# A trunk step on one core: the first twelve outputs of the first feed-forward stage summed in four quarters of the k tiles

## The chip, the cores and the metric

The kernel runs on one core of a Trainium2 chip. The metric is the device time of one execution in microseconds. The core has a matrix engine (TensorE, rows "PE", with its weight loads as "PEld"), a vector engine (VectorE, "DVE"), a scalar engine (ScalarE, "ACT"), GpSimd ("POOL") and a queue engine (SyncE, "SP"), on which nearly all transfers from memory are issued.

## What is computed

Two layers of a trunk over 256 tokens (128 of a context group, 128 of a latent group, d = 1024). A layer has three sub-layers: a feed-forward (SwiGLU, 2816 wide), a token mixer, and a second feed-forward; each is modulated by a condition and ends with a layer norm. The part at stake is the very first sub-layer:

```
mod = (silu(c) @ ada_w + ada_b)            # 9 rounds of 1024 columns per layer
h   = x * (1 + mod[scale]) + mod[shift]    # modulate
gate, up = split(h @ ffn1_w_in)            # k = 1024 = 8 tiles of 128
y   = (silu(gate) * up) @ ffn1_w_out
```

## The kernel before

**Work units.** The big products are a list of units, each up to 128x1024 of weights (512 KB), made by `_units` (line 129) and `_ffn_units` (line 47). In the first feed-forward unit ("g", f) holds the 8 k tiles of gate output f, ("u", f) those of up output f. A unit is loaded into one of 4 "raw" buffers (`ensure_dma`), split into a rounded part "hi" (ACT, line 520) and a rest "lo" (DVE, line 482) by `ensure_split`, and multiplied by `mmA`, which issues three TensorE instructions per k tile: hi with the rounded input, hi with its rest, lo with the rounded input. So a unit of 8 k tiles is 24 instructions. Five hi and five lo buffers let the split run three units ahead (`LEAD`).

**Start.** `setup` loads the condition, the 16 modulation tiles of the first two rounds (512 KB each, 16 buffers) and x in four pieces. `ada_start(q, A)` makes the modulation of two k tiles out of four modulation tiles: `strips` multiplies each as it comes, 8 products of 128 columns a tile on four 32-column strips of the array (bank D); then a copy by ACT, a transpose on TensorE (bank C), an add and a scale step on DVE. `build_u` then modulates x and splits it, per k tile. `first_four` runs the first four units k tile by k tile (four banks side by side), so that it can begin when two k tiles of the input are there; from the fifth unit on, a unit runs all its 8 k tiles in one go.

**Order.** Nothing runs in the order in which the code records it. `Program.order` is a list scheduler over all recorded operations with hand-set costs: a transfer of n bytes takes n/350 ns in one pipe after 1300 ns, and 700 ns more until it counts as landed; a TensorE product takes 109 ns; an operation with less time left until it is needed ("late") goes first. SP is free again 60 ns after an issue, so that in the plan a load is issued as soon as its buffer is free. What comes out is a fixed order for each engine, kept by the chip.

**Background work.** The other modulation rounds are partly summed on DVE ("d" pieces: two passes over a 128x1024 tile with the condition's row, line 486), from slot `D0` on; their row load (1 MB, `load_rows`) is issued at slot `GATE`, their tiles one slot each after that (`more_ada`), the rest of the constants at slot `GATE_C` (`late_loads`); all these loads wait for the newest "lo" (`gated`). The "k" pieces are strips on TensorE, some of them at the end of a sub-layer while the layer norm runs.

Of the kernel before, what the change touches and what calls it, by code (L numbers as in the profile page):

```python
# [16 lines left out]
P = 128  # L17
L = 2
D = 1024
KT = 8  # L20
# [22 lines left out]
def _r(c0, n=P):  # L43
    return list(range(c0, c0 + n))


def _ffn_units(s):
    wi, wo = f"ffn{s}_w_in", f"ffn{s}_w_out"
    k8 = list(range(KT))
    for f in range(FT):  # L50
# [78 lines left out]
def _units():  # L129
    out = []  # L130
    for l in range(L):
        for seq in (_ffn_units(1), _mix_units(), _ffn_units(2)):
# [122 lines left out]
DEP_ANY = 200  # L255
# [5 lines left out]


class Op:
    __slots__ = ("eng", "dur", "fn", "deps", "succ", "late", "due", "chain", "left", "ready", "nbytes", "pad")

    def __init__(self, eng, dur, fn, chain, due, nbytes, pad):
        self.pad = pad
        self.eng, self.dur, self.fn, self.chain, self.due, self.nbytes = eng, dur, fn, chain, due, nbytes
        self.deps, self.succ = set(), []
        self.late, self.left, self.ready = 1e18, 0, 0.0  # L270


class Program:
# [76 lines left out]
    def order(self):  # L350
# [15 lines left out]
        for i in range(len(ops) - 1, -1, -1):  # L366
            op = ops[i]
            late = end
            for j in op.succ:
                late = min(late, ops[j].late - _lat(op.eng, ops[j].eng))  # L370
            if not op.chain:
                k = bisect.bisect_right(slots, op.due)
                if k < len(slots) and first[slots[k]] > i:
                    late = min(late, ops[first[slots[k]]].late)
            op.late = late - op.dur
        free, now, later = {}, {}, {}
        for e in ("PE", "DVE", "ACT", "SP", "POOL"):
            free[e], now[e], later[e] = 0.0, [], []
# [6 lines left out]
        while len(out) < len(ops):  # L385
# [51 lines left out]
def _n(ap):  # L437
    n = 1
    for _, c in ap.ap[1:]:
        n *= c  # L440
    return n


class Recorder:
# [17 lines left out]
    def strips(self, items, start, stop):  # L462
        def fn():
            for out, lhsT, rhs in items:
# [3 lines left out]
        dur = sum(2 * max(107, _n(rhs) / 1.2) for _, _, rhs in items) / 4 + 70  # L468
        self.prog.add("PE", dur, fn, [x for _, a, b in items for x in (a, b)],
                      [o for o, _, _ in items] + ["strips"])  # L470
# [54 lines left out]
    def load(self, out, in_, queue="SP"):  # L525
        q = self.nc.sync if queue == "SP" else self.nc.gpsimd
        self.prog.add(queue, 60, lambda: q.dma_start(self.real(out), self.real(in_)), self.gate, [out], P * WORD * _n(out))

    def store(self, out, in_, queue="POOL"):
        q = self.nc.sync if queue == "SP" else self.nc.gpsimd  # L530
# [28 lines left out]
MIX_B = 60  # L559
MIXD_A = 48  # L560
MIXD_B = 80
D0 = 7


class Trunk:
# [106 lines left out]
    def ensure_dma(self, i):  # L672
        while self.n_dma <= min(i, len(self.units) - 1):
            k = self.n_dma
            n = self.units[k][3]
            self.raw[k] = self.t("raw", [UNIT])
            src = self.io["w"][self.offs[k]:self.offs[k + 1]].rearrange("(p n) -> p n", p=P)
            for a, b in self.cuts(k, n):
                self.nc.load(self.raw[k][:, a:b], src[:, a:b])
            self.n_dma += 1  # L680

    def ensure_split(self, i):
# [66 lines left out]
    def ada_load(self):  # L749
        while self.ada_free and self.ada_dma < min(len(self.plan), self.ada_limit):  # L750
            k = self.ada_dma
            if self.plan[k][0] > min(b for b in self.bubbles + [1e9] if b >= self.cur):
                self.ada_free = [b for b in self.ada_free if not b[1]]
                if not self.ada_free:
                    break
            buf = self.ada_free.pop(0)
            self.ada_t.append(buf)
            self.nc.load(buf[0], self.io["ada"][k * P * 1024:(k + 1) * P * 1024].rearrange("(p n) -> p n", p=P))
            self.ada_dma += 1

    def ada_extra(self, *bufs):
# [24 lines left out]
            self.ada_load()  # L786

    def ada_start(self, q, A):
        nc = self.nc
        ps = self.bank("D")  # L790
        for kk in range(4):
            w, buf = self.ada_take()
            for e in range(2):
                k = 2 * kk + e
                nc.strips([(ps[32 * j:32 * j + 32, q * P:(q + 1) * P], self.sil[:, k, :],
                            w[:, (e * 4 + j) * P:(e * 4 + j + 1) * P]) for j in range(4)], k == 0, k == KT - 1)
            self.ada_done(buf)
            self.ada_at += 1
        sb = self.t("adasb", [T])
        self.act(sb[:, 0:P], ps[:, q * P:(q + 1) * P], AF.Copy)  # L800
        tp = self.bank("C")[:, 0:P]
        nc.transpose(tp, sb[:, 0:P], self.kc("ident"))
        v = lambda x: x.rearrange("p (m f) g -> p m f g", m=2)[:, :, 2 * q:2 * q + 2, :]
        src = tp.rearrange("p (m f r) -> p m f r", m=2, f=2)[:, :, :, 0:2]
        bias = v(self.cv("adab", 0, 16).unsqueeze(2).to_broadcast([P, 16, 2]))
        self.tt(v(self.mod[:, 0:16, :]), src, bias, ALU.add)
        self.ts(A[:, 2 * q:2 * q + 2, :], self.mod[:, 8 + 2 * q:10 + 2 * q, :], 1.0, None, ALU.add)

    def ada_piece(self):
# [26 lines left out]
        else:  # L836
            if k == 0:
                self.half = 1 - self.half
            ps = self.bank("D")[:, self.half * T:(self.half + 1) * T]
            nc.strips([(ps[32 * j:32 * j + 32], self.sil[:, k, :], w[:, T * j:T * j + T]) for j in range(4)],  # L840
                      k == 0, k == KT - nd - 1)
            if k == KT - nd - 1:
                sb = self.t("adasb", [T])
                self.act(sb, ps, AF.Copy)
# [34 lines left out]
    def setup(self):  # L879
# [13 lines left out]
        nc.load(self.cols[:, cc0:cc0 + 16], io["cols"][:, cc0:cc0 + 16])  # L893
        i0, i1 = CONST["ident"]
        nc.load(self.const[:, i0:i0 + i1], io["const"][:, i0:i0 + i1])
# [3 lines left out]
        nc.load(self.cols[:, 0:16], io["cols"][:, 0:16])  # L899
        for f in range(0, KT, 2):  # L900
            nc.load(self.z[:, f:f + 2, :], io["x"][:, f:f + 2, :])
# [5 lines left out]
        A = self.t("A", [KT, 2])  # L907
        for q in range(4):
            self.ada_start(q, A)
        self.ada_flush()  # L910
        self.ensure_dma(N_RAW - 1)
        self.build_u(self.z, A, self.mods(0, 0), lambda f: None)
        self.next_ax(self.z, None)

    def gated(self, fn):

# [204 lines left out]
    def first_four(self, keys, evacs, rest=None):  # L1121
# [12 lines left out]
        for j in range(4):  # L1134
            self.ensure_split(base + 4 + (j > 0))
            self.end_slot(lambda j=j: evacs[j](pss[j]))

    def proj(self, ps, x, k0=0, ks=KT, off=0, start=True, stop=True):
# [11 lines left out]
    def ffn(self, l, s):  # L1150
# [18 lines left out]
            self.tt(ht[:, 1, :], h, ht[:, 0, :].bitcast(F32), ALU.subtract)  # L1169

        if l == 0 or s == 2:
            self.load_rows("sg", GATE, D0 - 1 if s == 1 else 2)
# [4 lines left out]
        self.first_four([("g", 0), ("u", 0), ("g", 1), ("u", 1)],  # L1177
                        [lambda ps: evac_g(0, ps), lambda ps: evac_u(0, ps),
                         lambda ps: evac_g(1, ps), lambda ps: evac_u(1, ps)])
        for f in range(2, FT):  # L1180
# [651 lines left out]
```

## Time and profile before

| | |
|---|---|
| median of 3 runs | 1397.91 us (1397.19 to 1398.42) |
| the profiled execution | 1396.16 us, of which the span 1394.4 us |
| PE busy | 1359.7 us (98%) |
| DVE busy | 1207.8 us (87%) |
| ACT busy | 769.5 us (55%) |
| moved by DMA | 326.60 MB, 234 GB/s on average |

The profile is of one execution. Busy time of an engine is the time that its instructions cover; a wait is idle time of an engine, put down to what ended it. Granted clock is the share of full speed that TensorE's clock was given in a stretch. "x2" in a row is the number of instructions merged into it.

### The profile page before, as it was taken

How to read it: one execution, taken by the hardware profiler on the slowest of the kernel's cores; microseconds unless marked ns; L12 is line 12 of the kernel's file. 1: busy time of each engine (PE TensorE's matmuls, PEld its weight loads, DVE VectorE, ACT ScalarE, POOL GpSimd, SP SyncE). 2: the span in 40 equal slices, each digit the busy share in tenths (PEclk: the TensorE clock that was granted, in tenths of full speed). 3: DMA queues.
4: the chain of work that ended last, by engine and by line, in shares of the span. 5: the costliest groups of instructions: out<-in, count | busy, mean ns of one | idle time of the engine just before them, and what ended most of it. 6: DMA issues, size and time to landing. Idle time of an engine off the chain costs nothing.

```text
span 1394.4 us, 28854 instructions
## 1 busy us (share of the span) xinstructions
PE 1359.7 (98%) x11488; PEld 1312.2 (94%) x11488; DVE 1207.8 (87%) x2299; ACT 769.5 (55%) x1265; POOL 13.6 (1%) x28
## 2 busy tenths in 40 slices
PE   7999999999999999999999999999999999999996
PEld 4999998999899989999989999899998999899996
DVE  3899998999999988999989999889999998865565
ACT  3655447566555557544465454675655455754542
POOL 0000000000100000000000000000000000000000
PEclk9999999999999999999999999999999999999998
DMA  9998976664567767889658886755455767476551
GB/s 349 341 325 291 333 269 211 211 209 145 183 220 249 243 242 272 280 290 340 232 194 304 284 307 234 241 175 178 137 174 184 257 224 257 139 224 195 179 191 57
DMA packets 92166, 326.60 MB, mean 234 GB/s; under 512 B 10944, under 2 KB 11360, under 8 KB 91392
## 3 DMA queue, kind: packets, MB, share of 16 engines
q1 hardware_dynamic: 90432, 319.88, 67.1%
q0 software_dynamic: 1600, 4.88, 1.1%
q8 instruction: 90, 1.47, 0.4%
q14 instruction: 44, 0.36, 0.1%
HBM read 321.28 MB, written 3.44 MB: 233 GB/s over the span
## 4 chain that ended last, share of the span: by engine, by line
PE 87%; DVE 7%; DMA 3%; ACT 2%; issue 1%; SPq 0%; DVEq 0%; ACTq 0%
PE bankm L460 63%; PE bankE L460 17%; DVE ring_lo L482 3%; PE bankA L460 2%; DVE T L486 2%; PE bankB L460 2%; PE bankC L460 2%; DMA T<-in_ada 1%; ACT ring_hi L520 1%; DMA ring_raw<-in_w 1%; DVE T L482 1%; DMA T<-in_x 1%; DMA ring_ada<-in_ada 0%; PE bankC L473 0%; DVE ring_w L482 0%
## 5 line engine op out<-in xcount | busy, mean ns | idle before, releaser
L520 ACT ACTIVATE ring_hi<-ring_raw 128x1024 fp32r<-128x1024 f32 (+2 forms) x462 | 477.0, 1037 | 332.4 <-PE bankm L460 141.9
L482 DVE TENSOR_TENSOR ring_lo<-ring_raw,ring_hi 128x1024 fp32r<-128x1024 f32 (+2 forms) x462 | 546.0, 1193 | 76.8 <-ACT ring_hi L520 75.9
L460 PE MATMUL bankm<-ring_U,ring_hi 128*128 128x256 f32 x3296 | 589.1, 280 | 6.3 <-ACT ring_hi L520 2.8
L460 PEld LDWEIGHTS bankm<-ring_U,ring_hi 128*128 128x128 f32 x3296 | 504.5, 189 | 11.3 <-ACT ring_U L520 4.0
L460 PE MATMUL bankm<-ring_U,ring_lo 128*128 128x256 f32 x1648 | 464.2, 282 | 0.2
L460 PEld LDWEIGHTS bankm<-ring_U,ring_lo 128*128 128x128 f32 x1648 | 311.7, 189 | 3.0 <-issue 1.3
L460 PE MATMUL bankm<-T,ring_hi 128*128 128x256 f32 x1464 | 254.7, 277 | 2.1 <-DVE T L482 2.1
L460 PEld LDWEIGHTS bankm<-T,ring_hi 128*128 128x128 f32 x1464 | 221.0, 188 | 3.2 <-issue 1.7
L460 PE MATMUL bankm<-T,ring_lo 128*128 128x256 f32 (+1 forms) x732 | 203.0, 277 | 0.0
L460 PE MATMUL bankE<-ring_U,ring_hi 128*128 128x256 f32 x832 | 147.4, 278 | 0.0
L460 PEld LDWEIGHTS bankm<-T,ring_lo 128*128 128x128 f32 x732 | 137.4, 188 | 0.0
L460 PEld LDWEIGHTS bankE<-ring_U,ring_hi 128*128 128x128 f32 x832 | 126.1, 189 | 0.4 <-issue 0.4
L486 DVE SCALAR_TENSOR_TENSOR T<-hp,cols,T 128x256 f32<-128x256 f32 x240 | 114.2, 481 | 3.8
L460 PE MATMUL bankE<-ring_U,ring_lo 128*128 128x256 f32 x416 | 115.5, 278 | 0.1
L460 PE MATMUL bankm<-ring_hi,ring_U 128*128 128x512 f32 x256 | 90.1, 419 | 0.0
L460 PE MATMUL bankE<-T,ring_hi 128*128 128x256 f32 (+1 forms) x488 | 86.7, 279 | 0.0
L520 ACT ACTIVATE ring_tB<-bankm 128x256 f32<-128x256 f32 x84 | 31.7, 382 | 96.1 <-PE bankm L460 96.0
L460 PEld LDWEIGHTS bankE<-ring_U,ring_lo 128*128 128x128 f32 x416 | 78.5, 189 | 0.5 <-DVE ring_lo L482 0.5
L486 DVE SCALAR_TENSOR_TENSOR ring_s<-ring_ada,ring_sg 128x1024 bf16<-128x1024 f32 (+2 forms) x68 | 74.4, 1094 | 2.8 <-DMA ring_ada<-in_ada 2.7
L460 PEld LDWEIGHTS bankE<-T,ring_hi 128*128 128x128 f32 x488 | 74.1, 188 | 1.0 <-DVE T L482 0.8
L486 DVE SCALAR_TENSOR_TENSOR ring_ada<-ring_ada,ring_sg 128x1024 f32<-128x1024 f32 (+2 forms) x68 | 73.9, 1094 | 0.1
L460 PE MATMUL bankE<-T,ring_lo 128*128 128x256 f32 (+1 forms) x244 | 67.9, 278 | 0.0
(263 smaller groups left out, 1602.6 us busy)
## 6 DMA issues: line engine op xcount, KB each, us to landing
ring_raw<-in_w SPq DMA_DIRECT2D x422, 512.0 KB, 4.5
ring_ada<-in_ada SPq DMA_DIRECT2D x107, 512.0 KB, 5.3
ring_raw<-in_w SPq DMA_DIRECT2D x32, 384.0 KB, 4.0
T<-in_ada SPq DMA_DIRECT2D x17, 512.0 KB, 7.8
ring_aa<-in_ada SPq DMA_DIRECT2D x10, 512.0 KB, 7.0
CM<-in_ada SPq DMA_DIRECT2D x6, 512.0 KB, 6.2
ring_sg<-in_crow SPq DMA_DIRECT2D x3, 1024.0 KB, 5.7
ring_raw<-in_w SPq DMA_DIRECT2D x8, 256.0 KB, 7.6
```

The costliest lines, as they stand in the source:

```text
L460: self.prog.add("PE", dur, lambda: self.nc.tensor.matmul(self.real(out), self.real(lhsT), self.real(rhs), start=start, stop=stop), [lhsT, ...
L482: self.dve(out, [in0, in1], lambda: self.nc.vector.tensor_tensor(out=self.real(out), in0=self.real(in0), in1=self.real(in1), op=op))
L486: self.dve(out, [in0, scalar, in1], lambda: self.nc.vector.scalar_tensor_tensor(out=self.real(out), in0=self.real(in0), scalar=self.real(s ...
L520: self.prog.add("ACT", dur, lambda: self.nc.scalar.activation(self.real(out), self.real(in_), func, **{k: self.real(v) for k, v in kw.item ...
```

## The change

The first twelve units (gate and up of outputs 0 to 5) are packed anew: unit ("p", q, b) holds the k tiles 2q and 2q+1 of four outputs (gate and up of f = 2b and 2b+1). Twelve such units, q outermost, take the place of the twelve old ones; the bytes and the number of TensorE products are the same. The sums of the 12 outputs stand in six banks through all four quarters, two outputs of 256 columns in a bank. Six 512-column products with a zero tile set these banks to zero at the start, and all later products add to them. `ada_start` now takes its four tiles together, with 16 products of 256 columns, two transposes and two adds. The loads of the start get a rank (a quarter's modulation tiles, its piece of x, its three units), which overrides "late". In the planner SP is busy until the planned pipe is no more than 3000 ns ahead. `GATE` goes from 2 to 9, `GATE_C` from 14 to 18, `D0` from 7 to 12, and the copies into `ax` become due later.

```diff
+FIRST_F = 6
-def _ffn_units(s):
+def _ffn_units(s, first=False):
...
+    if first:
+        for q in range(4):
+            for b in range(FIRST_F // 2):
+                yield ("p", q, b), [(wi, [2 * q, 2 * q + 1], _r(e * FF + f * P)) for f in (2 * b, 2 * b + 1) for e in range(2)]
+    for f in range(FIRST_F if first else 0, FT):
...
-GATE = 2
-GATE_C = 14
+GATE = 9
+GATE_C = 18
+AHEAD = 3000
...
+        for op in ops:
+            if op.rank is not None:
+                op.late = op.rank - end
...
-                free[e] = t + 60
                 pipe = max(pipe, t + 1300) + op.nbytes / 350.0
+                free[e] = max(t + 60, pipe - AHEAD)
...
-D0 = 7
+D0 = 12
...
     def ada_start(self, q, A):
         nc = self.nc
-        ps = self.bank("D")
-        for kk in range(4):
-            w, buf = self.ada_take()
-            for e in range(2):
-                k = 2 * kk + e
-                nc.strips([(ps[32 * j:32 * j + 32, q * P:(q + 1) * P], self.sil[:, k, :],
-                            w[:, (e * 4 + j) * P:(e * 4 + j + 1) * P]) for j in range(4)], k == 0, k == KT - 1)
+        ps = self.bank("D")[:, q % 2 * T:q % 2 * T + T]
+        took = [self.ada_take() for _ in range(4)]
+        nc.strips([(ps[32 * (2 * e + m):32 * (2 * e + m) + 32, :], self.sil[:, 2 * kk + e, :],
+                    took[kk][0][:, (2 * e + m) * T:(2 * e + m + 1) * T], kk == 0, kk == 3)
+                   for kk in range(4) for e in range(2) for m in range(2)])
...
+    def clear_banks(self):
+        zero = self.hp.rearrange("p f g t -> p (f g t)")[:, 0:512]
+        self.nc.memset(zero, 0.0)
+        for b in self.FIRST_BANKS:
+            self.nc.matmul(self.banks[b], zero[:, 0:P], zero, start=True, stop=False)
+
+    def first_quarters(self, evac_g, evac_u):
+        u = self.u
+        banks = [self.banks[b] for b in self.FIRST_BANKS]
+        for q in range(4):
+            for b in range(FIRST_F // 2):
+                fs = (2 * b, 2 * b + 1)
+                def mm(i):
+                    for kk in range(2):
+                        k = 2 * q + kk
+                        for j, f in enumerate(fs):
+                            for e in range(2):
+                                self.mmA(banks[f][:, e * T:(e + 1) * T], i, ((2 * j + e) * 2 + kk) * P, u[:, k, 0, :], u[:, k, 1, :],
+                                         False, k == KT - 1 and e == 1)
...
+                self.slot(("p", q, b), mm, evac if q == 3 else None)
```

## Rows read from the trace of the kernel before

**Rows 1.** Busy time by stretch: start:end and length, then busy time of PE, PEld, DVE, ACT, POOL, granted clock, DMA share, GB/s

```profile
0.00:5.00 5.00, 0.03 (x4) 0.06 (x5) 0.55 (x3) 1.50 (x2) 0.20 (x4) 1.00 0.55 178
5.00:10.00 5.00, 3.59 (x56) 2.14 (x60) 0.00 (x0) 0.00 (x0) 0.00 (x0) 1.00 0.99 374
10.00:15.00 5.00, 4.29 (x65) 2.21 (x57) 0.34 (x2) 0.28 (x1) 0.00 (x0) 1.00 1.02 364
15.00:20.00 5.00, 2.82 (x23) 2.18 (x24) 2.96 (x7) 4.20 (x11) 0.00 (x0) 1.00 1.03 408
20.00:25.00 5.00, 4.96 (x68) 3.77 (x67) 1.93 (x6) 1.17 (x3) 0.00 (x0) 1.00 1.03 414
25.00:30.00 5.00, 5.00 (x77) 3.84 (x70) 1.43 (x5) 1.82 (x7) 0.00 (x0) 1.00 1.03 410
30.00:35.00 5.00, 4.36 (x50) 2.91 (x49) 3.84 (x9) 4.86 (x13) 0.00 (x0) 1.00 0.83 293
35.00:40.00 5.00, 4.94 (x44) 4.83 (x43) 3.02 (x8) 3.90 (x8) 0.00 (x0) 1.00 0.87 305
...
50.00:60.00 10.00, 10.00 (x90) 10.00 (x90) 8.35 (x14) 7.25 (x10) 0.00 (x0) 1.00 1.03 413
60.00:210.00 150.00, 150.00 (x1323) 149.32 (x1321) 141.42 (x227) 74.60 (x99) 1.21 (x2) 1.00 0.88 303
```

**Rows 2.** Timeline of PE in the start: start, length, instruction, count, idle before

```profile
4.97 2.26 PE L465 MATMUL bankD<-T,sil 128*32 128x128 f32 x32 [4.97 <-DMA T<-in_ada]
...
9.63 1.08 PE L465 MATMUL bankD<-T,sil 128*32 128x128 f32 x16 [0.19 <-DMA T<-in_ada]
...
17.18 0.79 PE L460 MATMUL bankm<-ring_U,ring_hi 128*128 128x256 f32 x2 [2.37 <-ACT ring_hi L520]
...
20.63 0.40 PE L460 MATMUL bankm<-ring_U,ring_lo 128*128 128x256 f32 x1
...
31.70 0.64 PE L465 MATMUL bankD<-ring_ada,sil 128*32 128x128 f32 x16
...
39.50 0.39 PE L460 MATMUL bankA<-ring_U,ring_hi 128*128 128x256 f32 x2
39.72 0.28 PE L460 MATMUL bankA<-ring_U,ring_lo 128*128 128x256 f32 x1
```

**Rows 3.** Chain of waits in order of time, 0 to 80 us: start, length, what

```profile
12.71 8.14 DMA T<-in_ada
20.85 0.02 issue
20.86 8.80 DMA T<-in_x
```

**Rows 4.** Timeline of DVE in the start

```profile
1.25 0.17 DVE L511 MEMSET ones<- 128x128 f32 x1
12.63 0.17 DVE L482 TENSOR_TENSOR mod<-bankC,cols 128x8 f32<-128x8 f32 x1 [11.21 <-PE bankC L473]
12.83 0.17 DVE L492 TENSOR_SCALAR ring_A<-mod 128x4 f32<-128x4 f32 x1
```

**Rows 5.** Groups by shape, 190 to 260 us: a plain 512-column product (two instructions)

```profile
L460 PE MATMUL bankA<-ring_acc,ones 128*128 128x512 f32 x2 | 1.0, 593 | 0.0
```

**Rows 6.** Timeline of PE at the first layer norm

```profile
217.35 0.64 PE L465 MATMUL bankD<-ring_ada,sil 128*32 128x256 f32 x8 [2.59 <-DMA ring_ada<-in_ada]
...
219.52 0.41 PE L460 MATMUL bankm<-ring_U,ring_lo 128*128 128x256 f32 x1
```

**Rows 7.** The stretch behind that norm, columns as in rows 1

```profile
220.00:225.00 5.00, 5.00 (x37) 5.00 (x37) 4.79 (x14) 4.42 (x11) 0.00 (x0) 0.79 0.47 193
```

**Rows 8.** Timeline of PE again: the first transpose, and 24 strips of 256 columns

```profile
12.12 0.47 PE L473 MATMUL bankC<-const,ring_adasb 128*128 128x128 f32 x1
...
211.53 1.50 PE L465 MATMUL bankD<-ring_ada,sil 128*32 128x256 f32 x24
```

**Rows 9.** Timeline of ACT: from a modulation's copy to the rounded input

```profile
10.78 0.28 ACT L520 ACTIVATE ring_adasb<-bankD 128x128 f32<-128x128 f32 x1 [8.04 <-PE bankD L465]
15.67 0.49 ACT L520 ACTIVATE ring_tA<-T,mod,ring_A 128x128 f32<-128x128 f32 x1 [4.61 <-DMA T<-in_x]
16.19 0.42 ACT L520 ACTIVATE ring_U<-ring_tA 128x256 fp32r<-128x256 f32 x1
...
35.76 0.42 ACT L520 ACTIVATE ring_U<-ring_tA 128x256 fp32r<-128x256 f32 x1
```

**Rows 10.** Line 482, 40 to 210 us: splits on DVE, ns min/median/max

```profile
L482 DVE TENSOR_TENSOR ring_lo<-ring_raw,ring_hi x67: 949/1219/1228, 39.9 to 208.9; 128x1024 fp32r<-128x1024 f32 x59, 128x768 fp32r<-128x768 f32 x8
```

More of the change, by code (lines that the diff above doesn't have):

```diff
@@ L131, in _units @@
     for l in range(L):
-        for seq in (_ffn_units(1), _mix_units(), _ffn_units(2)):
+        for seq in (_ffn_units(1, l == 0), _mix_units(), _ffn_units(2)):
             for key, parts in seq:
@@ L263 @@
 class Op:
-    __slots__ = ("eng", "dur", "fn", "deps", "succ", "late", "due", "chain", "left", "ready", "nbytes", "pad")
+    __slots__ = ("eng", "dur", "fn", "deps", "succ", "late", "due", "chain", "left", "ready", "nbytes", "pad", "rank")
     def __init__(self, eng, dur, fn, chain, due, nbytes, pad):
-        self.pad = pad
+        self.pad, self.rank = pad, None
         self.eng, self.dur, self.fn, self.chain, self.due, self.nbytes = eng, dur, fn, chain, due, nbytes
@@ L460, in matmul, with strips @@
         self.prog.add("PE", dur, lambda: self.nc.tensor.matmul(self.real(out), self.real(lhsT), self.real(rhs), start=start, stop=stop), [lhsT, rhs], [out])
-    def strips(self, items, start, stop):
+    def strips(self, items):
         def fn():
-            for out, lhsT, rhs in items:
+            for out, lhsT, rhs, start, stop in items:
                 r = self.nc.tensor.matmul(self.real(out), self.real(lhsT), self.real(rhs), start=start, stop=stop)
             return r
-        dur = sum(2 * max(107, _n(rhs) / 1.2) for _, _, rhs in items) / 4 + 70
-        self.prog.add("PE", dur, fn, [x for _, a, b in items for x in (a, b)],
-                      [o for o, _, _ in items] + ["strips"])
+        dur = sum(2 * max(107, _n(rhs) / 1.2) for _, _, rhs, _, _ in items) / 4 + 70
+        self.prog.add("PE", dur, fn, [x for _, a, b, _, _ in items for x in (a, b)],
+                      [o for o, _, _, _, _ in items] + ["strips"])
     def transpose(self, out, in_, ident):
@@ L523, in table, with load @@
         self.prog.add("ACT", 1300, lambda: self.nc.scalar.preload_act_table_set(name), [], ["act_table"])
-    def load(self, out, in_, queue="SP"):
+    def load(self, out, in_, queue="SP", rank=None):
         q = self.nc.sync if queue == "SP" else self.nc.gpsimd
-        self.prog.add(queue, 60, lambda: q.dma_start(self.real(out), self.real(in_)), self.gate, [out], P * WORD * _n(out))
+        op = self.prog.add(queue, 60, lambda: q.dma_start(self.real(out), self.real(in_)), self.gate, [out], P * WORD * _n(out))
+        op.rank = rank
     def store(self, out, in_, queue="POOL"):
@@ L678, in ensure_dma @@
             for a, b in self.cuts(k, n):
-                self.nc.load(self.raw[k][:, a:b], src[:, a:b])
+                self.nc.load(self.raw[k][:, a:b], src[:, a:b], rank=k // 3 * 100 + 20 + k % 3 if k < 12 else None)
             self.n_dma += 1
@@ L757, in ada_load @@
             self.ada_t.append(buf)
-            self.nc.load(buf[0], self.io["ada"][k * P * 1024:(k + 1) * P * 1024].rearrange("(p n) -> p n", p=P))
+            slot = self.prog.slot
+            if k < 16:
+                self.quarter(k // 4)
+            self.nc.load(buf[0], self.io["ada"][k * P * 1024:(k + 1) * P * 1024].rearrange("(p n) -> p n", p=P),
+                         rank=k // 4 * 100 + k % 4 if k < 16 else None)
+            self.prog.slot = slot
             self.ada_dma += 1
@@ L789, in ada_start @@
         nc = self.nc
-        ps = self.bank("D")
-        for kk in range(4):
-            w, buf = self.ada_take()
-            for e in range(2):
-                k = 2 * kk + e
-                nc.strips([(ps[32 * j:32 * j + 32, q * P:(q + 1) * P], self.sil[:, k, :],
-                            w[:, (e * 4 + j) * P:(e * 4 + j + 1) * P]) for j in range(4)], k == 0, k == KT - 1)
+        ps = self.bank("D")[:, q % 2 * T:q % 2 * T + T]
[3 more added lines that the diff above has]
+                   for kk in range(4) for e in range(2) for m in range(2)])
+        for _, buf in took:
             self.ada_done(buf)
@@ L799, in ada_start @@
         sb = self.t("adasb", [T])
-        self.act(sb[:, 0:P], ps[:, q * P:(q + 1) * P], AF.Copy)
-        tp = self.bank("C")[:, 0:P]
-        nc.transpose(tp, sb[:, 0:P], self.kc("ident"))
+        self.act(sb, ps, AF.Copy)
+        tp = self.bank("C")[:, 0:T]
+        for b in range(2):
+            nc.transpose(tp[:, b * P:(b + 1) * P], sb[:, b * P:(b + 1) * P], self.kc("ident"))
         v = lambda x: x.rearrange("p (m f) g -> p m f g", m=2)[:, :, 2 * q:2 * q + 2, :]
-        src = tp.rearrange("p (m f r) -> p m f r", m=2, f=2)[:, :, :, 0:2]
+        part = tp.rearrange("p (b e m r) -> p e m b r", b=2, e=2, m=2)[:, :, :, :, 0:2]
+        out = v(self.mod[:, 0:16, :])
         bias = v(self.cv("adab", 0, 16).unsqueeze(2).to_broadcast([P, 16, 2]))
-        self.tt(v(self.mod[:, 0:16, :]), src, bias, ALU.add)
+        self.tt(out, part[:, 0], bias, ALU.add)
+        self.tt(out, out, part[:, 1], ALU.add)
         self.ts(A[:, 2 * q:2 * q + 2, :], self.mod[:, 8 + 2 * q:10 + 2 * q, :], 1.0, None, ALU.add)
@@ L839, in ada_piece @@
             ps = self.bank("D")[:, self.half * T:(self.half + 1) * T]
-            nc.strips([(ps[32 * j:32 * j + 32], self.sil[:, k, :], w[:, T * j:T * j + T]) for j in range(4)],
-                      k == 0, k == KT - nd - 1)
+            nc.strips([(ps[32 * j:32 * j + 32], self.sil[:, k, :], w[:, T * j:T * j + T], k == 0, k == KT - nd - 1)
+                       for j in range(4)])
             if k == KT - nd - 1:
@@ L892, in setup @@
         cc0 = COLS["cc"][0]
-        nc.load(self.cols[:, cc0:cc0 + 16], io["cols"][:, cc0:cc0 + 16])
+        nc.load(self.cols[:, cc0:cc0 + 16], io["cols"][:, cc0:cc0 + 16], rank=0)
         i0, i1 = CONST["ident"]
-        nc.load(self.const[:, i0:i0 + i1], io["const"][:, i0:i0 + i1])
+        nc.load(self.const[:, i0:i0 + i1], io["const"][:, i0:i0 + i1], rank=3)
         nc.table("silu_and_others")
@@ L898, in setup @@
         self.z = self.t("T1", [KT, T])
-        nc.load(self.cols[:, 0:16], io["cols"][:, 0:16])
+        nc.load(self.cols[:, 0:16], io["cols"][:, 0:16], rank=3)
         for f in range(0, KT, 2):
-            nc.load(self.z[:, f:f + 2, :], io["x"][:, f:f + 2, :])
+            self.quarter(f // 2)
+            nc.load(self.z[:, f:f + 2, :], io["x"][:, f:f + 2, :], rank=f // 2 * 100 + 10)
+        self.prog.slot = 0
         nc.memset(self.sil, 0.0)
@@ L907, in setup, with quarter @@
         A = self.t("A", [KT, 2])
+        self.clear_banks()
         for q in range(4):
+            self.quarter(q)
             self.ada_start(q, A)
         self.ada_flush()
+        self.prog.slot = 0
         self.ensure_dma(N_RAW - 1)
-        self.build_u(self.z, A, self.mods(0, 0), lambda f: None)
+        self.build_u(self.z, A, self.mods(0, 0), lambda f: self.quarter(f // 2))
+        self.prog.slot = 4 * FIRST_F
         self.next_ax(self.z, None)
+        self.prog.slot = 0
+    def quarter(self, q):
+        self.prog.slot = max(q * FIRST_F // 2 - 2, 0)
     def gated(self, fn):
@@ L1136, in first_four, with evac @@
             self.end_slot(lambda j=j: evacs[j](pss[j]))
+    FIRST_BANKS = ("m0", "m1", "m2", "E", "A", "B")
+    def clear_banks(self):
[16 more added lines that the diff above has]
+                                         False, k == KT - 1 and e == 1)
+                def evac():
+                    for f in fs:
+                        evac_g(f, banks[f][:, 0:T])
+                        evac_u(f, banks[f][:, T:2 * T])
+                self.slot(("p", q, b), mm, evac if q == 3 else None)
+        self.mmi = 0
     def proj(self, ps, x, k0=0, ks=KT, off=0, start=True, stop=True):
@@ L1176, in ffn @@
                 self.sched(GATE_C, lambda: self.gated(self.late_loads))
[L1177 to L1180, printed above, removed]
+        if l == 0 and s == 1:
+            self.first_quarters(evac_g, evac_u)
+        else:
+            self.first_four([("g", 0), ("u", 0), ("g", 1), ("u", 1)],
+                            [lambda ps: evac_g(0, ps), lambda ps: evac_u(0, ps),
+                             lambda ps: evac_g(1, ps), lambda ps: evac_u(1, ps)])
+        for f in range(FIRST_F if l == 0 and s == 1 else 2, FT):
             pg = self.bank("A" if f == 2 else None)
```

3 lines of the change are left out of this document (1 added, 2 removed).

## The prediction

> **What bounds the kernel now.** The page comes first: PE covers 98% of the span, so only a stretch in which PE idles or runs slowly can give anything. The table of stretches shows where that is. From 60 to 210 us PE is busy 150.00 of 150 us, whereas of the first 40 us it is idle some 10 us, while DMA is full (a share of 0.99 to 1.03, 364 to 414 GB/s from 5 to 30 us) [rows 1]. The timeline of PE shows what it does there: strips as modulation tiles land, the first main product at 17.18, strips up to 31.70, and the first unit that runs in one go at 39.50 [rows 2]. The chain of waits says what holds it: two transfers in a row, modulation tiles and a piece of x, 8.14 and 8.80 us long [rows 3]. So the start waits for 16 modulation tiles and x to land, and has only four units to work on meanwhile.
>
> The measure of the start is when the twelfth unit ends. The first four end at 39.50; a unit is 24 products, and a k tile (row of two and row of one) follows the next after 0.34 us, so 0.1133 us a product and 2.72 us a unit [rows 2]. Eight more end at 39.50 + 8 x 2.72 = 61.3. From there PE is full until the layer norm, so what the twelfth unit gains, the end gains, unless something behind gives it back.
>
> **The change, part by part.**
>
> *Transfers.* No bytes are added. A quarter is four tiles, a quarter of x and three units: 2.10 + 0.26 + 1.57 = 3.93 MB, at 410 GB/s 9.6 us. The tiles of the first quarter: by 10 us 2.76 MB had moved (178 and 374 GB/s over 5 us each), by which the fourth tile would be there at 8.4; before, PE waited for the fourth until 9.63 [rows 1, 2], so I take 9.6, or 1.2 us behind the count of bytes. Ahead of the last quarter's fourth tile come 13.96 MB; 10.74 had moved by 30 us, the rest at 412 GB/s takes 7.8, so 39.0 with the same 1.2. Before, the last tile was at work at 31.70 [rows 2]: the modulation is finished some 7 us later than now, and in return 72 products a quarter are there to cover the wait. On SP the ranks only reorder issues; in the plan a raw buffer is free before its turn (unit 4 needs the split of unit 0, planned at about 12 us, its turn comes some 9 us later), so I price this queue at nothing, covered by transfers in flight.
>
> The Trainium skill, "DMA: Bandwidth & Descriptors" (Where 436 GB/s comes from), names about 358 GB/s as what the memory side of a core can give. By it 3.93 MB would take 11.0 us a quarter. The trace disagrees with its 413 GB/s from 50 to 60 us [rows 1].
>
> *Clearing the banks.* Six products of 512 columns, on PE from about 1.7 us (the last memset ends at 1.42, one more follows) [rows 4]. The nearest row gives 1.0 us for one such product, a pair of instructions [rows 5]; in a stream a row overlaps the next by some 0.16 (0.28 long, 0.113 apart [rows 2]), so 0.84 each, 5.0 in all, at the level of that row. The other end is the clock. The granted clock reads 1.00 from the start [rows 1], but a tile of strips takes 1.08 us at 9.63 and 0.64 at 31.70, and a single main product shows 0.40 at 20.63, 0.28 at 39.72 [rows 2]; at the first layer norm, where PE had waited 2.59 us, a product shows 0.41, just ahead of a stretch granted 0.79 [rows 6, 7]. The durations decide: I read the start, with PE idle before it, as the lower level (1.2 GHz), and the long run of main products as 2.4 GHz. All six at the lower level take 10.1 us and end at 11.8. I take three of each, 7.6 us, ending at 9.3: just under the tiles, so no charge; both ends stay for the range.
>
> *Strips.* 32 instructions of 256 columns where there were 64 of 128. 24 take 1.50 us [rows 8], so 32 some 1.9. They now wait for all four tiles, so all 1.9 lie behind the last landing, where 0.64 to 1.08 lay before [rows 2].
>
> *From strips to the first product.* Before: the strips end at 10.71, the copy starts at 10.78, the transpose costs 0.47, add and scale step run from 12.63 to 13.00, modulation and rounding take 0.52 and 0.42 [rows 2, 4, 8, 9]. Without the transpose's wait behind other strips that is 2.4 us; a longer copy, a transpose more and an add more bring 0.5. In the last quarter it took from 32.34 to the end of rounding at 36.18, 3.8 us, with ACT and DVE splitting weights in between [rows 2, 9]. Bounds 2.4 and 3.9; I take 3.3, nearer the crowded row because three units are split in every quarter.
>
> *The pace.* First main product at 9.6 + 1.9 + 3.3 = 14.8. After that PE keeps the planned order. The plan moves 350 bytes a ns, so 11.2 us a quarter, more than the chip needs, and strips stand in the order where the plan expects their tiles: by its constants the strips of the second quarter are ready at 19.8 us and the first main product at about 14, so 53 of the 72 products go first; in the next quarters 54 and 55. A quarter costs 54 x 0.1133 = 6.1, plus 1.9 and 3.3, 11.3 us; the other 18 products cover 2.0 of the 3.3. The twelfth unit ends at 14.8 + 3 x 11.3 + 72 x 0.1133 = 56.9. Against 61.3 that is **4.4 us less**.
>
> *What the cover must still do.* DVE was busy 149.8 of the 160 us from 50 to 210 [rows 1]. Behind the new twelfth unit some five splits more are done than at 50 before, 6.1 us [rows 10]; 143.7 us of work remain for the 148.7 us from 56.9 to 205.6. That fits, with 5 us to spare: no charge, but if DVE falls behind, PE waits for "lo". The row load and the first pieces of the background work wait for later slots, as does `late_loads`; DMA has room for them (a share of 0.88 [rows 1]). The evacuations of six outputs come in one bunch, but the next unit needs only the first bank, free two units (5.4 us) earlier. What is late next is the modulation of quarters two to four, by the plan's pace: 1.3 us of PE idle each.
>
> *The planner's SP.* It reorders issues in all of the kernel. After 60 us PE's only long wait for a load is 2.59 us at the first layer norm [rows 6]. Bounds: that 2.6 saved, or rival three; I take zero, as the order could move the load either way.
>
> **Sum.** The profiled execution, 1396.2 (span 1394.4 and 1.8 around it), becomes 1391.8; the median stands 1.7 above it, so **1393.5**. Less than 0.2%, 2.8 us, can't be told from no change.
>
> **Rivals.**
> 1. *PE's own work paces the start.* If strips stand early enough in the order to hide the whole chain, the floor is 14.8 + 4 x 8.16 + 3 x (1.9 + 0.5 of transposes) = 54.6: 6.7 us less, **1391.2**; with the 2.6 of the layer norm 1388.6. For it: tiles land before their planned place. Against: the order is fixed.
> 2. *The clock holds the first quarter.* All six clears at the lower level end at 11.8, the strips at 1.08 a tile at 16.1, first main product at 19.4, and the twelfth unit ends at 61.5, or, with the crowded chain (3.9, so 11.9 a quarter), 63.8: 0.2 to 2.5 us more, **1398.1 to 1400.4**, mostly no change. For it: ten microseconds of strips had not raised the level before [rows 2]. Against: 512 columns without a gap are denser work than strips.
> The Trainium skill, "TensorE: Matmul & The Clock Gate" (What's actually happening), says that the throttled state is the default and activity releases it. By that rule the clears begin at the lower level; the durations of the first strips agree [rows 2].
> 3. *Slower: tiles late at the layer norms.* With SP held back in the plan, the modulation tiles wanted at a norm are issued behind weights. Five norms have work behind them; PE already waits 2.59 us at the first [rows 6]. Two 512 KB loads ahead of the tile cost 2 x 1.27 us at 413 GB/s [rows 1], five times 12.7; less 4.4 that is 8.3 more, **1406.2**. It decides from 0.9 us a norm on. Against: with DMA at 0.88 the plan is seldom 3 us ahead.
>
> **How the numbers follow.** Forecast 0.50 (its own range 1390.5 to 1396; 0.43 of it beyond 2.8 us, 0.07 within), rival one 0.21, rival two 0.17 (taken as no change), rival three 0.12. Faster 0.43 + 0.21 = 0.64; same 0.07 + 0.17 = 0.24; slower 0.12. The range runs from 1388.5 (rival one with the norm's wait) to 1399.5 (most of rival two); it leaves out rival three and the ends of the others.
>
> **What would show it.** Right: the twelfth unit's end at 56 to 59; the first main product near 15; strips in one run of 32 instructions with 53 to 55 products of the quarter before them; PE idle some 1.3 us ahead of each quarter; PE full behind. Wrong: clears past 11 us (rival two), no idle between quarters (rival one), PE waiting for modulation tiles at the norms (rival three), PE waiting for "lo" after 60 us (the cover gone).

## The result and the profile after

The changed kernel takes 1407.09 us, median of 4 runs (1406.7 to 1407.54), the one before 1398.11 beside it (1397.19 to 1398.42): a ratio of 1.007 [1.0054, 1.0087]. It is slower by some 9 us, where 4.4 us less was forecast, and lies outside the range. The page, line of busy time (share of the span) and instructions:

```profile
PE 1367.6 (97%) x11376; PEld 1316.1 (94%) x11376; DVE 1207.6 (86%) x2304; ACT 769.4 (55%) x1265; POOL 13.6 (1%) x28
```

DVE and ACT do what they did; PE is 7.9 us longer at work and the span 10.5 us longer (1404.9), so PE works more slowly somewhere and waits elsewhere. To see where, count the main products in PE's timeline and note when the N-th ended, in both kernels (us; 288 products are twelve units, 1560 to 1632 is the first layer norm):

| main product | before | after | after is later by |
|---|---|---|---|
| 24 | 24.62 | 21.57 | -3.0 |
| 72 | 36.94 | 29.36 | -7.6 |
| 144 | 45.10 | 41.82 | -3.3 |
| 216 | 53.26 | 56.43 | 3.2 |
| 288 | 61.42 | 65.50 | **4.1** |
| 1560 | 206.07 | 210.16 | 4.1 |
| 1632 | 225.45 | 235.25 | **9.8** |
| the last | 1380.18 | 1390.69 | 10.5 |

Two places make the loss: the start (4.1 us, of which nothing is lost or won again in the 145 us behind it) and the first layer norm (5.7 us). The other 0.7 is the net of steps of at most 1.6 us behind it. PE's timeline in the start, with the idle time before a row and what ended it, against [rows 2]:

```profile
1.73 5.49 PE L469 MATMUL bankm<-hp 128*128 128x512 f32 x6 [1.73 <-DVE hp L520]
...
8.89 1.02 PE L469 MATMUL bankB<-hp 128*128 128x512 f32 x2
9.84 1.93 PE L474 MATMUL bankD<-T,sil 128*32 128x256 f32 x32
13.37 0.44 PE L482 MATMUL bankC<-const,ring_adasb 128*128 128x128 f32 x2 [1.60 <-ACT ring_adasb L529]
16.07 1.18 PE L469 MATMUL bankm<-ring_U,ring_hi 128*128 128x256 f32 x2 [2.25 <-ACT ring_U L529]
17.04 0.41 PE L469 MATMUL bankm<-ring_U,ring_lo 128*128 128x256 f32 x1
...
30.28 0.38 PE L469 MATMUL bankm<-ring_U,ring_hi 128*128 128x256 f32 x1 [0.93 <-ACT ring_U L529]
31.17 0.38 PE L469 MATMUL bankm<-ring_U,ring_hi 128*128 128x256 f32 x1 [0.51 <-DVE ring_U L491]
36.02 1.07 PE L474 MATMUL bankD<-T,sil 128*32 128x256 f32 x16
36.91 1.05 PE L474 MATMUL bankD<-CM,sil 128*32 128x256 f32 x16
39.93 0.38 PE L482 MATMUL bankC<-const,ring_adasb 128*128 128x128 f32 x2
43.27 0.38 PE L469 MATMUL bankm<-ring_U,ring_hi 128*128 128x256 f32 x1 [1.45 <-ACT ring_U L529]
44.10 0.38 PE L469 MATMUL bankm<-ring_U,ring_hi 128*128 128x256 f32 x1 [0.45 <-DVE ring_U L491]
...
57.14 0.39 PE L469 MATMUL bankm<-ring_U,ring_hi 128*128 128x256 f32 x1 [0.44 <-DVE ring_U L491]
```

The six zero products run from 1.73 to 9.9, the strips in one run of 32 behind them, and PE waits for the modulated input (ring_U) ahead of the first three quarters and behind the first product of the last three. The quarters begin at 16.07, 30.28, 43.27 and 56.31, some 13 to 14 us apart. The 0.41 of the single product at 17.04 is the slow row of [rows 6], not the 0.28 of [rows 2]. The stretches around two such waits and the norm, columns as in [rows 1]:

```profile
15.00:20.00 5.00, 3.92 (x16) 3.62 (x17) 3.71 (x9) 2.82 (x7) 0.00 (x0) 0.50 1.03 406
45.00:50.00 5.00, 5.00 (x42) 4.52 (x45) 1.22 (x1) 0.09 (x1) 0.00 (x0) 0.67 0.69 214
225.00:230.00 5.00, 3.30 (x28) 1.33 (x21) 4.79 (x10) 2.98 (x8) 0.00 (x0) 0.58 1.00 358
```

The granted clock is 0.50 in the first quarter, 0.67 in the third: half of full speed, 1.2 GHz, for all or most of the stretch. In the first PE had idled 1.60 and 2.25 us, in the third 1.45 and 0.45. What makes the waits long is seen best on DVE, between the transposes of the third quarter and its first products:

```profile
40.35 0.17 DVE L491 TENSOR_TENSOR mod<-bankC,cols 128x8 f32<-128x8 f32 x1 [5.48 <-PE bankC L482]
40.55 0.16 DVE L491 TENSOR_TENSOR mod<-mod,bankC 128x8 f32<-128x8 f32 x1
40.63 1.23 DVE L491 TENSOR_TENSOR ring_lo<-ring_raw,ring_hi 128x1024 fp32r<-128x1024 f32 x1
41.78 0.16 DVE L501 TENSOR_SCALAR ring_A<-mod 128x4 f32<-128x4 f32 x1
41.97 0.60 DVE L501 TENSOR_SCALAR ring_tA<-T,ring_A,mod 128x128 f32<-128x128 f32 x2
42.49 1.22 DVE L491 TENSOR_TENSOR ring_lo<-ring_raw,ring_hi 128x1024 fp32r<-128x1024 f32 x1
43.63 0.75 DVE L491 TENSOR_TENSOR ring_U<-ring_tA,ring_U 128x256 fp32r<-128x256 f32 x2
```

Two splits of 1.23 us stand inside the chain, the first between the sum (mod) and its scale (ring_A), the second ahead of the rest of the rounded input. DVE had idled 5.48 us before: it is the order that puts them there. Then the norm, on PE, on DVE and on SP's queue (which issues ten modulation tiles in a row there):

```profile
221.67 1.07 PE L474 MATMUL bankD<-ring_ada,sil 128*32 128x256 f32 x16
223.35 0.64 PE L474 MATMUL bankD<-ring_ada,sil 128*32 128x256 f32 x8 [0.61 <-DMA ring_ada<-in_ada]
224.64 0.64 PE L474 MATMUL bankD<-ring_ada,sil 128*32 128x256 f32 x8 [0.65 <-DMA ring_ada<-in_ada]
226.74 1.08 PE L474 MATMUL bankD<-ring_ada,sil 128*32 128x256 f32 x8 [1.46 <-DMA ring_ada<-in_ada]
228.06 1.08 PE L474 MATMUL bankD<-ring_ada,sil 128*32 128x256 f32 x8 [0.24 <-DMA ring_ada<-in_ada]
229.08 0.58 PE L469 MATMUL bankE<-ring_U,ring_lo 128*128 128x256 f32 x1
```
```profile
227.71 2.35 DVE L491 TENSOR_TENSOR ring_lo<-ring_raw,ring_hi 128x1024 fp32r<-128x1024 f32 x2
```
```profile
215.27 14.26 SPq L536 DMA_DIRECT2D ring_ada<-in_ada  x10
```

By the row of waits alone PE would seem to wait for modulation tiles, as in rival three. But these strips are background work; the product at 229.08 reads "lo", which DVE began only at 227.71 and ended at 228.92, behind the norm's work, although ACT had begun the "hi" halves at 214.56 and 216.31. In the kernel before DVE had made them ahead of the norm:

```profile
207.60 2.49 DVE L482 TENSOR_TENSOR ring_lo<-ring_raw,ring_hi 128x1024 fp32r<-128x1024 f32 x2 [2.11 <-ACT ring_hi L520]
...
210.53 1.22 DVE L482 TENSOR_TENSOR ring_lo<-ring_raw,ring_hi 128x1024 fp32r<-128x1024 f32 x1
```

So the planner filled the gap with strips whose tiles were not there yet. The trace alone can't say which of the two held PE: the split and the last of these strips end within some 0.2 us of each other. The reading to be tested: it is the place of one split in the order, not the tiles.

### The profile page after: what moved, and what is told of

It is laid out like the page before. It is cut to its first block, busy times and chain, and to the rows that moved or that the text cites. A ratio compares the mean times of both kernels' runs of the same rounds, so it can differ in the third digit from the quotient of the medians.

```text
span 1404.9 us, 28625 instructions
## 1 busy us (share of the span) xinstructions
PE 1367.6 (97%) x11376; PEld 1316.1 (94%) x11376; DVE 1207.6 (86%) x2304; ACT 769.4 (55%) x1265; POOL 13.6 (1%) x28
## 4 chain that ended last, share of the span: by engine, by line
PE 89%; DVE 7%; DMA 2%; ACT 1%; issue 1%; SPq 0%; DVEq 0%; ACTq 0%
PE bankm L469 65%; PE bankE L469 17%; DVE ring_lo L491 2%; PE bankB L469 2%; PE bankA L469 2%; PE bankC L469 2%; DVE T L495 2%; DVE T L491 1%; DMA T<-in_x 1%; PE bankD L474 0%; DMA ring_raw<-in_w 0%; DVE ring_w L491 0%; PE bankC L482 0%; ACT ring_hi L529 0%; DMA T<-in_ada 0%
```

## The experiments

Each kernel is the changed one with the edit shown (e8: the kernel before). Ratios are to the kernel before, run on the same chip. First all numbers (us of main products as above):

| kernel | 288th | 1560 to 1632 | last | ratio to before |
|---|---|---|---|---|
| before | 61.42 | 19.4 | 1380.2 | |
| after | 65.50 | 25.1 | 1390.7 | 1.007 [1.0054, 1.0087] |
| e1 one split first | 64.91 | 16.9 | 1379.6 | 1.0006 [0.9991, 1.0021] |
| e2 planned pipe 370 | 61.26 | 22.0 | 1381.8 | 0.9993 [0.9979, 1.0006] |
| e3 planned pipe 380 | 60.32 | 25.8 | 1386.3 | 1.004 [1.0028, 1.0052] |
| e4 chain first, pipe 400 | 58.43 | 18.6 | 1376.5 | 0.9992 [0.9978, 1.0007] |
| e5 chain first alone | 61.61 | 26.8 | 1387.7 | one run, 1403.68 |
| e6 no clears (on e1) | 64.70 | 18.3 | 1382.4 | one run, 1398.49 |
| e7 e4 without idle in quarter one | 57.67 | 21.1 | 1378.8 | 0.9978 [0.9964, 0.9991] |
| e8 before, with the hold on SP | 61.05 | 16.0 | 1377.7 | 0.9989 [0.9974, 1.0003] |
| e9 e1 without idle in quarter one | 63.05 | 18.2 | 1380.5 | 1.0 [0.9985, 1.0014] |
| e10 e7, background strips later | 56.97 | 17.9 | 1381.6 | 1.0027 [1.0013, 1.0041] |

The times of main products are of one execution each, and executions of one kernel differ by several us: that of e4 was its fastest (1392.5 for a median of 1396.35), that of e7 its slowest (1394.82 for 1393.58). So whole kernels are compared by the ratio alone.

**The norm: one split, or the tiles?** e1 ranks a single DVE operation first.

```diff
                 self.tt(lo[:, a:b], raw[:, a:b], hi[:, a:b].bitcast(F32), ALU.subtract)
+                if k in (71,):
+                    self.prog.ops[-1].rank = 0
```

> The changed kernel with one DVE instruction put first in its queue: the 'lo' of unit 71, the mixer's fourth, which the changed order puts behind the whole work of the first layer norm. Theory A (order): of the 9 us lost, 4.2 are lost in the start (twelfth unit at 65.5 instead of 61.3) and 5.7 at the first norm, because that one split stands late in DVE's order; so the 72 products from the 1560th to the 1632nd take about 19 us again instead of 25.1, and the time is 1400.5 to 1402.5; the twelfth unit stays at 65.5. Theory B (transfers): the modulation tiles and weights land late at the norm whatever the order; PE waits as long for them and the time is 1406 to 1408.

The stretch fell from 25.1 to 16.9 us, further than the 19 expected, and the time to no measurable difference from before; the start stayed nearly as it was (64.91). Its DVE, PE and SP's queue at the norm:

```profile
215.16 1.22 DVE L491 TENSOR_TENSOR ring_lo<-ring_raw,ring_hi 128x1024 fp32r<-128x1024 f32 x1
```
```profile
219.63 0.39 PE L469 MATMUL bankm<-ring_U,ring_hi 128*128 128x256 f32 x1 [0.17 <-ACT ring_U L529]
220.31 0.64 PE L474 MATMUL bankD<-ring_ada,sil 128*32 128x256 f32 x8 [0.29 <-DMA ring_ada<-in_ada]
```
```profile
214.67 3.35 SPq L536 DMA_DIRECT2D ring_ada<-in_ada  x4
```

"lo" is made near the start of the norm's work, the products run on without waiting for it, and of the waits for tiles 0.29 us is left. So the place of that split was the cause, together with what the planner arranges around it: with the one rank it also rewrote the other queues, and SP issues four modulation tiles in a row there instead of ten. How much of the 8.2 us belongs to the split alone, no run parts. e2 and e3 change only the planner's figure for the pipe (370 and 380), to see whether that place is luck:

```diff
-                pipe = max(pipe, t + 1300) + op.nbytes / 350.0
+                pipe = max(pipe, t + 1300) + op.nbytes / 370.0
```

> The changed kernel with one number of the planner changed, the rate of its pipe, 370 instead of 350 bytes a ns; no transfer changes but in order. In its order the split of unit 71 stands ahead of the norm again. Theory A: the norm's 5.7 us come back and the strips stand a little earlier (quarters of 10.6 us in the plan instead of 11.2), so 1397.5 to 1401. Theory B (transfers late at the norm, or the plan's hold on SP): 1404.5 to 1407.

> The same with 380 bytes a ns. In its order the split of unit 71 stands behind the norm, as in the changed kernel. Theory A: the start is up to 1 us better than at 370, yet the time is 4 to 6 us longer than at 370: 1402.5 to 1406. Theory B: equal to 370 or up to 1 us shorter.

A constant moved by 3%, from 370 to 380, turned the order over. The same split in e2, then in e3:

```profile
210.03 1.21 DVE L491 TENSOR_TENSOR ring_lo<-ring_raw,ring_hi 128x1024 fp32r<-128x1024 f32 x1
```
```profile
222.52 2.35 DVE L491 TENSOR_TENSOR ring_lo<-ring_raw,ring_hi 128x1024 fp32r<-128x1024 f32 x2
```

e3 has the better start (60.32 for 61.26) and is slower, as its split stands behind the norm again. e2 pays a wait for a tile there instead, a longer one than that of [rows 6]:

```profile
217.76 1.08 PE L474 MATMUL bankD<-ring_ada,sil 128*32 128x256 f32 x8 [3.44 <-DMA ring_ada<-in_ada]
```

**The hold on SP.** e8 puts only that part of the change into the kernel before.

```diff
-                free[e] = t + 60
                 pipe = max(pipe, t + 1300) + op.nbytes / 350.0
+                free[e] = max(t + 60, pipe - 3000)
```

> The kernel before with nothing changed but SP's hold in the planner (busy until the pipe is no more than 3000 ns ahead). Theory A (the hold is not what costs the time): no wait at any norm grows by over 1 us and the time is within 2 us of before. Rival three of the prediction (the hold puts tiles behind weights at the norms): 4 us or more above before, with PE waiting for modulation tiles at the norms.

No loss: 16.0 us at the norm where before took 19.4, without the tile's wait of [rows 6]. Holding loads back does not make tiles late in the kernel before, and e1, which keeps the hold, has 0.29 us of such waits at the norm. In the changed kernel itself PE waits for no tile behind 240 us, where rival three had four more norms to lose at: its mechanism falls.

**The start: order of the chain, clock, or clears?** e5 ranks the operations from strips to modulated input ahead of the splits, e4 does so with the planned pipe at 400.

```diff
+            n = len(self.prog.ops)
             self.ada_start(q, A)
+            self.urgent(n, q * 100)
...
+        n = len(self.prog.ops)
         self.build_u(self.z, A, self.mods(0, 0), lambda f: self.quarter(f // 2))
+        self.urgent(n, 50)
...
+    def urgent(self, n, rank):
+        for op in self.prog.ops[n:]:
+            if not op.nbytes:
+                op.rank = rank
```

> The changed kernel with the planner's pipe at 400 bytes a ns, and with every operation that turns modulation tiles into the modulated input (strips, copy, transposes, adds, modulation and its split) put first in its queue. Theory A: the splits no longer stand in front of that chain (4.3 to 6 us from the end of the strips to the first product, now about 3.5), strips stand earlier, the norm's order is good: the twelfth unit ends at 57 to 60 and the time is 1393 to 1397, below the kernel before. Theory C (the start is held by the tiles' landing or by the clock, not by the order): the twelfth unit ends at 62 to 65 and the time is 1398 to 1402.

> The changed kernel with only the chain from modulation tiles to modulated input put first in its queues; the planner's pipe stays at 350. It is read by its start alone (its order at the norm is the bad one). Theory A (two parts of equal weight, order of the chain and place of the strips): the chain is 1 to 2 us shorter in the last two quarters, and the twelfth unit ends at 62 to 63.5 (65.5 in the changed kernel, 58.4 with both). Theory B (the place of the strips alone, which the rate sets): it ends at 65 to 66. Theory C (the chain alone): at 58 to 60.

The chain's order alone gives 3.9 us at the twelfth unit (65.50 to 61.61), somewhat more than expected, both together 7.1. From the strips' end to the first product it now takes 3.5 us in each of the last three quarters. In e5 the third quarter, and the stretch in which the clock had been 0.67:

```profile
41.98 0.38 PE L469 MATMUL bankm<-ring_U,ring_hi 128*128 128x256 f32 x1 [0.25 <-DVE ring_U L491]
```
```profile
45.00:50.00 5.00, 5.00 (x61) 3.95 (x59) 0.00 (x0) 0.79 (x2) 0.00 (x0) 1.00 0.57 189
```

Without the wait of 1.45 us the clock stays at full speed: here a wait on a split cost twice, once as idle time and once in the clock behind it. e5 as a whole stays slow, with the bad order at the norm (26.8 us there). e6 takes the clears away (the first product into a bank carries the start flag, the other half of the bank gets none):

```diff
-        self.clear_banks()
...
-                                         False, k == KT - 1 and e == 1)
+                                         k == 0 and e == 0, k == KT - 1 and e == 1)
```

> The changed kernel with the one split first (as e1), and without the six clearing products: the first product into a bank starts it, the other half of the bank starts by overwriting. The clears left out, nothing else. Theory A (the clears cost nothing, the tiles come no earlier): strips of the first quarter begin within 0.5 us of 9.8 but take longer than 1.93 us, as PE has not run before them and is at its lower level; the first main product comes 0 to 2 us later than with the clears and the twelfth unit ends at 64.5 to 66.5. Theory B (the clears hold the first quarter): strips begin near 8.5 and the twelfth unit ends 1 us or more earlier, at 63 to 64.

```profile
5.58 2.26 PE L474 MATMUL bankD<-T,sil 128*32 128x256 f32 x16 [5.58 <-DMA T<-in_ada]
8.38 1.08 PE L474 MATMUL bankD<-T,sil 128*32 128x256 f32 x8 [0.55 <-DMA T<-in_ada]
9.85 1.08 PE L474 MATMUL bankD<-T,sil 128*32 128x256 f32 x8 [0.39 <-DMA T<-in_ada]
```

PE takes the fourth tile at 9.85, as it lands, and the clears had ended at 9.9: 0.2 us at the twelfth unit, nothing more. e7 adds to e4 four products of 512 columns with zeros, one behind the strips and three behind the transposes of the first quarter, in the two gaps of PE; e9 adds them to e1.

```diff
+        if q in (0,):
+            self.fill(1)
...
+        if q in (0,):
+            self.fill(3)
...
+    def fill(self, n):
+        zero = self.hp.rearrange("p f g t -> p (f g t)")[:, 0:512]
+        at = len(self.prog.ops) - 1
+        for _ in range(n):
+            self.nc.matmul(self.banks["B"], zero[:, 0:P], zero, start=False, stop=False)
+            self.prog.ops[-1].deps.add(at)
```

> e4 with four more zero products of 512 columns in the first quarter, one behind the strips and three behind the transposes, into a bank where they add zero, so that PE is not idle in the two gaps before the first main product (1.5 and 3.1 us in e4). Theory A (the gaps let the clock fall, and the first 24 products run at half of it): they run at 0.28 us a row from the start, the granted clock stays 1.00 from 14 to 21 us, the 24th product ends at 19 to 20 instead of 21.46, and the twelfth unit at 56 to 57 instead of 58.4; time 1.5 to 2.5 us below that of e4. Theory B (the level there follows something else, or the zero products count as no work): the 24th product at 21 or later, the twelfth unit at 58 to 59.5, time as e4 or 1 us above.

> The changed kernel with the one split ahead of the norm (as in e1) and four zero products in quarter one's two gaps, nothing else. Theory A (the lower clock of the first products costs the start as much as they run longer): the 24th main product ends 1.2 us earlier than in e1 (20.93), at 19.5 to 20, and the 12th unit at 63.5 to 64.2 for e1's 64.91, so the time is 0.7 to 1.4 us below e1's ratio of 1.0006, at 0.9990 to 0.9998. Theory B (the next quarter waits for its own modulation, so the minute won in quarter one is lost in the wait ahead of quarter two): the 12th unit at 64.7 to 65.1 and the same ratio as e1.

e7, PE's timeline and the stretch that had been at 0.50:

```profile
11.24 1.12 PE L469 MATMUL bankB<-hp 128*128 128x512 f32 x2
13.33 0.44 PE L482 MATMUL bankC<-const,ring_adasb 128*128 128x128 f32 x2 [0.96 <-ACT ring_adasb L529]
13.60 2.74 PE L469 MATMUL bankB<-hp 128*128 128x512 f32 x6
16.84 0.85 PE L469 MATMUL bankm<-ring_U,ring_hi 128*128 128x256 f32 x2 [0.49 <-ACT ring_U L529]
```
```profile
15.00:20.00 5.00, 4.43 (x28) 3.16 (x27) 3.75 (x8) 2.56 (x7) 0.00 (x0) 1.00 1.02 405
```

Work without use keeps the clock at full speed here: the first 24 products end at 20.22 for 21.46 in e4, the twelfth unit 0.8 us sooner, both a little less than expected. In e9 the same four products give 1.8 us at the 24th (19.17 for 20.93) and all of it is still there at the twelfth unit, against the theory that the next quarter's wait would swallow it. Its end shows none of it: by the 1632nd product 0.6 us is left, and the ratio can't be told from e1's. In the two traces a lower clock goes with it: the granted clock is 0.83 in e9 and 1.00 in e1 from 215 to 225 us, at the norm, and the same again from 705 to 715. e7 is faster than the kernel before by 0.2%.

**A version beyond e7?** e10 keeps the background strips behind the products of their slot, so that they can't fill a gap early.

```diff
+        if op.chain:
+            self.newest = i
...
+            n = len(self.prog.ops)
...
+            if not self.ada_closing:
+                self.prog.ops[n].deps.add(self.prog.newest)
```

> e7 (chain operations first, planned pipe at 400 bytes a ns, zero products in quarter one) with the background strips held behind the last product of the slot in which they are recorded. Start as in e7: 12th unit at 57.5 to 58.0. Theory A (what the first norm costs is set by the order of instructions that the planner happens to write there, as loads and splits fall): the stretch from product 1560 to 1632 is 16 to 19 us where e7 has 21.1, and the time is 2 to 5 us below the kernel before (ratio 0.9965 to 0.9985). Rival (the norm gives back what the start gains, because the loads that stand ahead of the modulation tile need their time anyway): 20 to 22 us again, ratio 0.998 or above.

The norm fell to 17.9 us, as expected, but the time did not: it was to fall below the kernel before and is 0.3% above it. After 2000 main products e10 was still 4.0 us ahead of e7 (265.35 for 269.34). The gain went behind that, where PE waits in the token mixer for DVE. PE's timeline there, in e7 and then in e10:

```profile
273.80 1.93 PE L474 MATMUL bankD<-ring_ada,sil 128*32 128x256 f32 x32
276.57 0.59 PE L469 MATMUL bankm<-T,ring_hi 128*128 128x384 f32 x2 [0.83 <-DVE T L491]
```
```profile
273.16 0.59 PE L472 MATMUL bankm<-T,ring_hi 128*128 128x384 f32 x2 [3.27 <-DVE T L494]
281.65 0.64 PE L477 MATMUL bankD<-ring_ada,sil 128*32 128x256 f32 x8
```

In e7 32 background strips fill that wait. In e10 the wait is empty, and its strips stand between main products, eight at a time (281.65, 309.23, 335.58, 360.82, 391.80), where each row of eight holds the products up. DVE does not take the lead away: e10 is still 3.4 us ahead of e7 at the end of the wait, and 0.4 behind at the 2600th product. So holding the strips back lost the place where they were free; that is read from the two traces, and no run puts just those strips back.

## Why the prediction was wrong, step by step

**Right.** The transfers: the fourth tile is there at 9.85 (e6) for 9.6, and no quarter waits for a load. The clears: 8.1 us for 7.6, ending with the tiles, at no charge (e6). The strips: one run of 1.93 us for 1.9. The cover: from 60 to 205 us PE waits for nothing, so the start's result is kept to the norm as forecast, though DVE had done only 24.81 us of work in the first 60 us (30.24 before):

```profile
0.00:60.00 60.00, 50.62 (x389) 40.01 (x390) 24.81 (x51) 26.38 (x49) 0.20 (x4) 0.91 0.83 298
```

**"From strips to the first product", sized 3.3.** It took 4.3, 3.8, 5.3 and 5.4 us in the four quarters (strips' end to first product), above the crowded bound of 3.9 in three of them. The crowded row was seen, but taken as the far end: with three units split in every quarter, splits stood inside the chain, as the edit ranked only loads; with the chain ranked (e5) it took 3.5. In the first quarter it is most of why the first main product comes at 16.07 instead of 14.8.

**"The pace", 11.3 us a quarter.** The number of products ahead of the strips was 51, 42 and 28, not 53 to 55, so more of each later chain was covered. By this luck PE's idle time in the rows behind the first product comes to 3.8 us, as forecast (three times 1.3). What the sum lacked is the clock. The first 24 products took 5.5 us (16.07 to 21.57) where 0.1133 each gives 2.7; of the 2.8 us more the clock makes 2.0, with k tiles 0.64 apart instead of 0.34, and the rest is a wait of the second product for the rest of the rounded input. Some 1.6 more went in the third quarter, where k tiles stood 0.64 apart from 45.15 on. Counted from start to start of the main products, the 8.6 us between the forecast 56.9 and 65.50 are: the clock 3.7, waits for the modulated input 1.9 (5.7 in all for 3.8, more than the rows' idle time because a quarter's second product waits too), the first product 1.3, three pairs of transposes 0.7 (priced only in rival one), strips 0.5 (a run of 32 holds the products up by 2.1, not 1.9); 0.5 is left over in small gaps.

**Rival two** had the clock, but in the wrong place: it let the clears and the first strips run slowly and took the products behind them as fast. The clears did raise the clock (the first three took 5.49 us, the last ones 1.02 each); behind the idle gaps that the chain itself makes it fell again. Its 61.5 to 63.8 for the twelfth unit lay nearer than the forecast. The Trainium skill, "TensorE: Matmul & The Clock Gate" (HAM oscillation — how this bites in real kernels), describes a kernel whose wait for the next transfer throttles the engine again and again, so that the next products start slowly. The trace agrees in kind: 0.50, 0.67 and 0.58 in the three stretches shown, each with waits in it or just ahead, but not for every wait, as the second quarter shows (0.93 and 0.51 us, and products 0.34 a k tile behind).

**Rival one's** floor, 8.16 + 2.3 us a quarter, is what e7 runs at: 10.5 us from the 144th to the 216th product (38.98 to 49.51). The packing can do what was expected of it; as it was planned it did not.

**"The planner's SP", taken as zero.** This step failed most, with 5.7 us. Its bounds were made for the resource that the edit touches, late or early loads. The fixed order of all engines is written anew when any cost or rank moves, and what moved was one split on DVE, with the strips and loads around it. The list of signs had it, as PE waiting for "lo", but for a DVE that falls behind; here it was the order of DVE's work that put the split last. Rival three's 1406.2 came close to the measured time by luck: e8 shows its mechanism to be harmless, and e1 that one rank undoes the loss with the hold in place.

## What to carry to other kernels

Where a planner writes one fixed order for all engines, an edit to ranks or costs rewrites the places that it doesn't mention: after such a change, compare when each fixed share of the main products ends, and look at every step in that difference before judging the edit itself. A chain that the matrix engine waits for should be ranked ahead of bulk work on every engine that it crosses, since a wait costs idle time and can cost, behind it, products at half the clock. And a wait's named releaser is not its cause when the engine was only given filling work: look for what the next main product reads.

## What the runs showed that was not expected

The clock falls after short gaps: 1.45 and 0.45 us without work, with a full stretch of products before them, were followed by products 0.64 us apart per k tile (0.67 granted), while 0.93 and 0.51 in the second quarter of the same execution were not (1.00). In e1, e6 and e9 the same 1.45 and 0.45 us were followed by k tiles 0.64 us apart too. Four idle-time products with zeros, 3.9 us of PE's time in the first quarter of e7, bought back 1.2 us there. And a planner's constant changed from 370 to 380 bytes a ns moved the median by 7.9 us (1395.23 to 1403.08).
